# Two layers of a hybrid backbone on one core: where chunks, weight blocks and late queries stand in the order of the program

## The chip, the cores and the metric

The program runs on one core of one Trainium2 chip. The metric is the time of one execution on the device, in microseconds; the medians below are of three timed runs. One further execution was taken with the hardware profiler, and all rows below come from it.

## The reference

It computes two layers on 1024 latent tokens and 128 context tokens of width 1024, 1152 in all. Each layer normalizes its input, scales and shifts it by values from a conditioning vector, runs a mixer, and adds the gated, normalized result to the input. Cut to the names that matter:

```python
def even_mixer(h, w_in, ...):            # layer 0
    p = h @ w_in
    qa, ka, va, oa, gates, qb, kb, vb, z = split(p)
    ha = rmsnorm(mlstm(qa, ka, va, gates, forward) + mlstm(..., backward)) * sigmoid(oa)   # 4 heads of 128
    hb = block_attend(rope(rmsnorm(qb)), [rope(rmsnorm(kb)), ctx_k], [vb, ctx_v])          # 8 query heads of 64 over 2 key heads
    return (concat(ha, hb) * silu(z)) @ w_out

def odd_mixer(h, w_in, rpb, w_out, ...): # layer 1
    q, k, v, z = split(h @ w_in)         # 16 heads of 64
    o = na_attend(q, k, v, ctx_k, ctx_v, rpb)   # 8 x 16 window of the grid and all context keys, one softmax
    return (o * silu(z)) @ w_out

for layer in range(2):
    h = rmsnorm(x) * (1 + scale) + shift
    x = x + gate * rmsnorm(mixer(h))
```

The outputs are both token groups after the two layers, the mLSTM states, and the keys and values of the context.

## The kernel before

**Tiling.** The 1152 tokens are three chunks of 384 columns (`CW`), the width of 1024 eight blocks of 128 (`KB`). Each operand of the projections is split into a high and a low part (`hh`, `hl` for activations, `whi`, `wlo` for weights), and a product is three matmuls per k: high by high, high weights by low activations, low weights by high activations. `feat_part` (L362 to L369) issues these for one chunk; a block of 128 output columns for one chunk is a group of 24 matmuls of 384 columns in one PSUM bank, then evicted by one of the functions `evs` (q, k, v, o, z). The 16 gates of the mLSTM have their own group of 16 matmuls (`gates_proj`, L395 to L417).

**Buffers.** SBUF tiles of one tag rotate. Almost everything large has the tag "u", a pool of 35 slots: activations, weight halves, queries, bias tables, softmax rows. Raw weights land in two "raw" buffers, are cast by ScalarE (ACT) to `whi`, and GpSimd (POOL) or VectorE (DVE) subtracts to get `wlo` (`weights`, L121; `split`, L110). The PSUM banks are: pj two, s three, and tr, ptr and o one each.

**Order.** A planner orders the instructions of each engine by a simulated time, with the order of tracing as priority; the grouped-query attention alone has TensorE's order written out by hand. Slots of a tag are given out in the order of tracing, so what is traced earlier has its slots earlier. DMAs wait in SP's queue, or in that of another engine, in order.

**Phases.** *front*: for k = 0 to 7 the modulation of block k (`mod_first`), the normalization of chunk 0's block k (`norm_cols`) and then, for chunk 0, the gates and four weight blocks of head 0 (q, k, v, o), each in an own bank (`acc`: o, three of s, tr). The column statistics (`rms_cols`, L286 to L312) of chunk 1 are computed at k = 5, those of chunk 2 after the loop. `later(c, bs)` then computes blocks bs of chunk c in the pj banks, block 0 being the gates. *a*: the gate chain (`gates`, L419 and after: transposes, cumulative sums and maxima of the gates over all tokens, a pass through DRAM, exponentials into `e`), the rest of head 0, its z block and head 1's first blocks. *mlstm*: four heads. *g*: queries, keys and values of the grouped-query attention, `gqa_q` (L851). *gqa*: units of two query tiles, ten turns of transposes each (`gqa_turn`), apply, gate; `w_out(0, k)` is loaded between. *out0*: output projection of layer 0 and the normalization for layer 1; it loads y back from DRAM through the raw buffers (`load_y`). *na*: eight pairs of heads, `na_proj(p)` (projections) and `na_pair(p)` (attention, nine units); blocks in `late` are projections of the same pair that are put between its units. Pairs 1, 3 and 5 compute the values of two pairs at once from `w_v`. The last part of the output projection runs beside pair 7.

**Names of the change.** `turned` (L871) transposes the queries of one tile and casts them; for the second group g = 1 the calls of tiles 7 and 8 are put off into `self.turned` and popped in the first unit of `gqa`. `w_out(l, j)` (L1075) loads a block of the output weights; its second argument to `weights` says which engine subtracts ("lo" is DVE, "" is POOL). `W(b)` in `na_proj` (L1114) loads block b of pair p (0 q, 1 k, 2 v, 3 z).

## Time and profile before

| | us |
|---|---|
| median of three timed runs (lowest and highest 1527.02 and 1527.52) | 1527.03 |
| the profiled execution | 1527.66 |
| its span, first to last instruction | 1525.9 |
| PE busy in the span | 1489.1 |
| PE weight loads busy | 1370.8 |
| DVE busy | 828.0 |
| ACT busy | 711.9 |
| POOL busy | 449.3 |

The span is the profiler's time from the first to the last instruction; 1.76 us of that execution lie outside. Busy times are sums of durations of each engine; weight loads run beside matmuls. A matmul's end is modelled, so that durations of matmuls that follow each other overlap. In a timeline row the bracket gives the idle time of the engine before the instruction and the instruction or DMA that ended it.

### The profile page before, as it was taken

To read this page: it belongs to the slowest core of one execution; us is meant where nothing else is said; L and a number is where in the kernel's file an instruction comes from. 1 tells how busy PE (TensorE), PEld (TensorE's weight loads), DVE (VectorE), ACT (ScalarE), POOL (GpSimd) and SP (SyncE) were. 2 spreads that over 40 slices of the span, in tenths; PEclk is the share of its full clock that TensorE was granted. 3 is DMA by queue.
4 is the path that set the end of the run, shared out by engine and by line. 5 is a ranking of instruction groups with operands and counts; after the bars stand their busy time and mean duration, and the time that the engine had idled before them with its cause. 6 is when DMAs were issued, how large, how long until landed. Compare 5 with 4: busy or idle time off the path is not lost.

```text
span 1525.9 us, 27070 instructions
## 1 busy us (share of the span) xinstructions
PE 1489.1 (98%) x10139; PEld 1370.8 (90%) x10139; DVE 828.0 (54%) x2387; ACT 711.9 (47%) x1767; POOL 449.3 (29%) x644
## 2 busy tenths in 40 slices
PE   7899999999999999999999999999999999999998
PEld 5799999999999888887888989999999999988786
DVE  5833887963457766665565352535344434445532
ACT  4533535263445777786454352534344344345411
POOL 0001202011135655675224141323132222233200
PEclk9999999999999999999999999999999999999999
DMA  9203546332311000122423222131213121125342
GB/s 378 79 15 130 190 147 239 137 122 75 111 48 44 1 32 24 44 67 70 151 98 137 74 62 80 42 98 31 85 38 104 33 82 69 54 90 167 106 131 83
DMA packets 73284, 143.80 MB, mean 94 GB/s; under 512 B 15737, under 2 KB 44609, under 8 KB 73153
## 3 DMA queue, kind: packets, MB, share of 16 engines
q1 hardware_dynamic: 68566, 126.91, 25.0%
q10 hardware_dynamic: 4586, 15.16, 2.7%
q8 instruction: 80, 1.31, 0.3%
q14 instruction: 52, 0.42, 0.1%
HBM read 115.47 MB, written 21.86 MB: 90 GB/s over the span
## 4 chain that ended last, share of the span: by engine, by line
PE 49%; DMA 1%; DVE 1%; ACT 1%; POOL 1%; issue 0%; DVEq 0%; POOLq 0%; ACTq 0%
PE pj L367 7%; PE pj L368 7%; PE pj L369 7%; PE pj L383 6%; PE pj L382 6%; PE pj L384 6%; PE o L1290 4%; PE s L1267 3%; PE ptr L107 2%; PE tr L107 2%; DMA y<-yd 1%; POOL wlo L116 1%; DMA raw<-in_w_out_dram 0%; DVE sb L1273 0%; POOL pr L925 0%
## 5 line engine op out<-in xcount | busy, mean ns | idle before, releaser
L367 PE MATMUL pj<-hh,whi 128*128 128x384 f32 x1168 | 400.2, 343 | 1.8 <-ACT qT L102 1.2
L368 PE MATMUL pj<-hl,whi 128*128 128x384 f32 x1168 | 397.0, 340 | 0.0
L369 PE MATMUL pj<-hh,wlo 128*128 128x384 f32 x1168 | 395.8, 339 | 0.5 <-DVE wlo L116 0.4
L367 PEld LDWEIGHTS pj<-hh,whi 128*128 128x128 f32 x1168 | 219.6, 188 | 5.5 <-ACT qT L102 1.8
L369 PEld LDWEIGHTS pj<-hh,wlo 128*128 128x128 f32 x1168 | 219.4, 188 | 1.9 <-DVE wlo L116 0.9
L368 PEld LDWEIGHTS pj<-hl,whi 128*128 128x128 f32 x1168 | 219.6, 188 | 1.2
L1277 POOL TENSOR_SCALAR sb<-sb,sm 128x512 f32<-128x512 f32 (+1 forms) x128 | 85.1, 671 | 247.7 <-DVE sm L1276 238.7
L116 POOL TENSOR_TENSOR wlo<-raw,whi 128x1024 fp32r<-128x1024 f32 x43 | 103.0, 2400 | 132.8 <-ACT whi L115 113.7
L925 POOL TENSOR_SCALAR pr<-pr,smg 128x384 f32<-128x384 f32 x192 | 110.0, 591 | 73.9 <-PE pj L107 41.0
L382 PE MATMUL pj<-whi,hh 128*128 128x256 f32 x432 | 122.5, 284 | 0.3 <-DVE nr L783 0.3
L383 PE MATMUL pj<-wlo,hh 128*128 128x256 f32 x432 | 122.5, 284 | 0.0
L384 PE MATMUL pj<-whi,hl 128*128 128x256 f32 x432 | 122.2, 283 | 0.0
L382 PE MATMUL pj<-whi,yh 128*128 128x512 f32 x288 | 114.3, 397 | 2.9 <-DVE o L1085 1.5
L916 DVE CUSTOM_DVE_ANT_0 pr<-s,zero 128x384 f32<-128x384 f32 x192 | 103.8, 553 | 24.3 <-PE s L915 20.9
L383 PE MATMUL pj<-wlo,yh 128*128 128x512 f32 x288 | 113.9, 395 | 0.0
L1275 ACT ACTIVATE sb<-sb,sm 128x512 f32<-128x512 f32 (+1 forms) x128 | 88.9, 695 | 52.9 <-DVE sm L1273 49.3
L384 PE MATMUL pj<-whi,yl 128*128 128x512 f32 x288 | 113.3, 394 | 0.0
L915 PE MATMUL s<-Kst,Q 128*128 128x384 f32 x384 | 107.8, 372 | 1.1 <-ACT pt L1035 1.1
L254 DVE CUSTOM_DVE_ANT_0 mj<-wm,cb 128x512 f32<-128x512 f32 x128 | 89.5, 699 | 5.2 <-DMA wm<-in_w_modT_dram 3.0
L115 ACT CAST whi<-raw 128x1024 fp32r<-128x1024 f32 x77 | 79.7, 1046 | 19.5 <-DMA raw<-in_w_v_dram 6.6
L1273 DVE CUSTOM_DVE_ANT_1 sb<-s,bias 128x512 f32<-128x512 f32 (+1 forms) x112 | 72.9, 664 | 24.9 <-PE ptr L107 12.1
L382 PEld LDWEIGHTS pj<-whi,hh 128*128 128x128 f32 x432 | 81.3, 188 | 1.4 <-issue 0.5
(350 smaller groups left out, 2901.3 us busy)
## 6 DMA issues: line engine op xcount, KB each, us to landing
wm<-in_w_modT_dram SPq DMA_DIRECT2D x32, 512.0 KB, 5.2
raw<-in_w_c_dram SPq DMA_DIRECT2D x25, 512.0 KB, 3.5
raw<-in_w_ab_dram SPq DMA_DIRECT2D x20, 512.0 KB, 3.5
e<-rbd ACTq DMA_DIRECT2D x12, 768.0 KB, 7.7
bias<-in_na_bias_dram SPq DMA_DIRECT2D x16, 576.0 KB, 4.1
wm<-in_w_mod_dram SPq DMA_DIRECT2D x16, 512.0 KB, 9.8
raw<-in_w_out_dram SPq DMA_DIRECT2D x16, 512.0 KB, 3.6
y<-yd SPq DMA_DIRECT2D x18, 448.0 KB, 3.4
```

The lines of the kernel that those rows point to most:

```text
L116: (eng_lo or nc.gpsimd).tensor_tensor(lo, src, hi.bitcast(F32), ALU.subtract)
L254: nc.vector.tensor_tensor_reduce(junk, w[:, b, :], cb[:, r, :], 1.0, 0.0, ALU.mult, ALU.add, mp[:, hf, q // 4, 2 * (q % 4) + b, r : r + 1])
L367: nc.tensor.matmul(ps[:, :CW], a, hh, start=k == 0, stop=False)
L368: nc.tensor.matmul(ps[:, :CW], a, hl, start=False, stop=False)
L369: nc.tensor.matmul(ps[:, :CW], b, hh, start=False, stop=k == KB - 1)
L382: nc.tensor.matmul(ps[:, :width], hh, a, start=k == 0, stop=False)
L383: nc.tensor.matmul(ps[:, :width], hh, b, start=False, stop=False)
L384: nc.tensor.matmul(ps[:, :width], hl, a, start=False, stop=k == KB - 1)
L915: nc.tensor.matmul(s[:, :CW], x, y, start=part == 0, stop=part == 1)
L916: nc.vector.tensor_tensor_reduce(pr[:, c, :], s[:, :CW], zero, -1.0, -NEG, ALU.add, ALU.min, m3[:, c : c + 1])
L925: nc.gpsimd.tensor_scalar(pr[:, c, :], pr[:, c, :], r, 0.5, ALU.mult, ALU.mult)
L1275: nc.scalar.activation(x, x, AF.Exp, bias=nm, scale=-1.0, accum_out=r)
```

## The change

It has five parts.

1. *Front.* In the per-k loop chunk 0 has three weight blocks instead of four. After the loop chunk 1's gates and q block are computed in two passes, k = 0 to 3 for both, then k = 4 to 7 for both, each in a pj bank. Then chunk 0's fourth block (o) is computed in its bank, then k, v and o of chunk 1, then the gates of chunk 2; in phase a q and k of chunk 2, then v and o. Before, the order was gates, q, k of chunk 1, gates of chunk 2, in phase a q and k of chunk 2, v of both chunks, o of both. `rms_cols` of chunk 2 is traced after the rest of `norm_cols` of chunk 1 instead of ahead of it.
2. *Late queries.* `turned` of tiles 7 and 8 of the second group takes a bank of tag s instead of ptr or tr, and the two calls are popped at turns 7 and 9 of the first unit instead of 5 and 7.
3. *Output weights of layer 0.* For j = 6 and 7 DVE subtracts instead of POOL.
4. *Values of pair 1.* The two weight blocks of `w_v` are loaded and split at the end of `na_proj(0)`, ahead of `na_pair(0)`, instead of in `na_proj(1)`.
5. *Pair 7.* Blocks v, q and z of pair 7 are loaded and split at the end of `na_proj(6)`, ahead of `na_pair(6)`, instead of in `na_proj(7)`.

```diff
--- before.py
+++ after.py
@@ -869,7 +869,7 @@
                 Q.append(self.u([P, 2, 4, P], F32R, n="Q"))
 
             def turned(i=i, q=q, Qt=Q[-1]):
-                pt = self.ps(("tr", "ptr")[i % 2])[:, :256]
+                pt = self.ps("s" if g and i in (7, 8) else ("tr", "ptr")[i % 2])[:, :256]
                 for j in range(2):
                     self.flipped(pt[:, j * P : (j + 1) * P], q[:, 2 * j : 2 * j + 2].rearrange("p a b -> p (a b)"))
                 for hh in range(2):
@@ -994,7 +994,7 @@
                 next(steps, None)
                 next(steps, None)
                 for n, _ in enumerate(turns):
-                    if (j, i, n) in ((0, 0, 5), (0, 0, 7)):
+                    if (j, i, n) in ((0, 0, 7), (0, 0, 9)):
                         self.turned.pop(0)()
                     if i == 4 and n == 7 or i == 6 and n == 5:
                         next(ctx)
@@ -1074,7 +1074,7 @@
 
     def w_out(self, l, j):
 
-        return self.weights(self.a["w_out"][l, j], ("", "lo")[j % 2] if l else "")
+        return self.weights(self.a["w_out"][l, j], "lo" if (j % 2 if l else j >= 6) else "")
 
     def out_half(self, y, w, n, o, ss, gg):
         nc = self.nc
@@ -1109,9 +1109,12 @@
             self.nc.sync.dma_start(raw, self.a["w_c"][4 * p + b])
         return self.weights(self.a["w_c"][4 * p + b], raw=raw)
 
+    def v_weights(self, p):
+        return [self.weights(self.a["w_v"][p // 2, :, q * D : (q + 1) * D]) for q in range(2)]
+
     def na_proj(self, h, p, w):
         nc, a = self.nc, self.a
-        W = lambda b: self.na_weights(p, b)
+        W = lambda b: self.w7[b] if p == 7 and b in self.w7 else self.na_weights(p, b)
         two = lambda t: t[2 * p : 2 * p + 2].rearrange("h t d -> t h d")
         v2 = lambda t: t.rearrange("p (h d) -> p h d", d=DHB)
 
@@ -1181,7 +1184,7 @@
             self.feat(h, W(2), vev)
         elif p % 2:
 
-            w = [self.weights(a["w_v"][p // 2, :, q * D : (q + 1) * D]) for q in range(2)]
+            w = self.wv if p == 1 else self.v_weights(p)
             for i in range(NT):
                 ps = self.tok(h, i, lambda k: tuple(x[:, (k % 4) * 256 : (k % 4 + 1) * 256] for x in w[k // 4]), 256)
                 nc.scalar.copy(v[:, i, :], ps[:, :P])
@@ -1211,6 +1214,11 @@
             self.feat(h, w, kev)
 
             late = [lambda w=w, e=e, c=c: self.feat(h, w, e, [c]) for w, e, c in [(wq, qev, 2), (wz, zev, 2)]]
+
+        if p == 0:
+            self.wv = self.v_weights(1)
+        if p == 6:
+            self.w7 = {b: self.na_weights(7, b) for b in (2, 0, 3)}
 
         def terms(hh, j, k0, n):
 
@@ -1357,7 +1365,7 @@
                 if k + 1 < KB:
                     self.mod_first(k + 1, wm[k + 1])
                 self.norm_cols(h, 0, xt[0], rms[0], [k])
-                for b in range(NB + 1):
+                for b in range(3 + 1):
                     part[b](acc[b], 0, [k])
 
                 if k == 5:
@@ -1365,10 +1373,10 @@
                 if k > 5:
                     self.norm_cols(h, 1, xt[1], rms[1], range(3 * k - 18, 3 * k - 15))
             ends = [gend, *evs[:NB]]
-            for b in range(NB + 1):
+            for b in range(3 + 1):
                 ends[b](0, acc[b][:, :CW])
+            self.norm_cols(h, 1, xt[1], rms[1], range(6, KB))
             rms.append(self.rms_cols(xt[2]))
-            self.norm_cols(h, 1, xt[1], rms[1], range(6, KB))
             self.norm_cols(h, 2, xt[2], rms[2], range(KB))
 
             def later(c, bs):
@@ -1377,16 +1385,23 @@
                     part[b](ps, c, range(KB))
                     ends[b](c, ps[:, :CW])
 
-            later(1, (0, 1, 2))
+            ps = [self.ps("pj") for _ in range(2)]
+            for ks in (range(KB // 2), range(KB // 2, KB)):
+                for b in range(2):
+                    part[b](ps[b], 1, ks)
+            for b in range(2):
+                ends[b](1, ps[b][:, :CW])
+            for b in range(3 + 1, NB + 1):
+                part[b](acc[b], 0, range(KB))
+                ends[b](0, acc[b][:, :CW])
+            later(1, (2, 3, 4))
             later(2, (0,))
         with self.phase("a"):
             self.gates(gT)
             self.c0 = [self.load_c0(hd) for hd in range(2)]
             self.nall = self.const([P, 8], "nall")
             later(2, (1, 2))
-            for b in range(3, NB + 1):
-                for c in (1, 2):
-                    later(c, (b,))
+            later(2, (3, 4))
             blocks(0, evs, (4,), lambda n: self.t(n, 1, [P, D], F32R))
             nxt, evs = self.mlstm_proj(1)
             blocks(1, evs, (0, 1))
```

## Rows read from the trace of the kernel before

**Rows 1.** The page, busy time of each engine over the span: us, share, instructions.

```profile
PE 1489.1 (98%) x10139; PEld 1370.8 (90%) x10139; DVE 828.0 (54%) x2387; ACT 711.9 (47%) x1767; POOL 449.3 (29%) x644
```

**Rows 2.** The table of stretches: window, its length in us, then the busy us of PE, PEld, DVE, ACT and POOL with their instructions, the granted clock of PE, the share of the DMA engines and GB/s. The first is the later half of the front, the second the start of grouped-query attention.

```profile
61.00:75.00 14.00, 12.38 (x69) 10.87 (x69) 12.98 (x40) 8.24 (x21) 0.00 (x0) 1.00 0.05 10
...
514.00:524.00 10.00, 6.52 (x48) 5.05 (x48) 6.71 (x26) 9.58 (x21) 7.83 (x14) 1.00 0.00 0
```

**Rows 3.** The timeline of PE in the front, 49 to 75 us: start, duration, engine, line, operation, out<-in, form and count, and in brackets the idle time before it and what ended it.

```profile
49.62 0.33 PE L368 MATMUL pj<-hl,whi 128*128 128x384 f32 x1
...
49.80 0.34 PE L369 MATMUL pj<-hh,wlo 128*128 128x384 f32 x1
...
51.67 0.39 PE L408 MATMUL o<-hh,wg 128*64 128x384 f32 x1 [1.54 <-ACT hh L325]
...
53.61 0.39 PE L409 MATMUL o<-hl,wg 128*64 128x384 f32 x1 [0.50 <-DVE hl L326]
...
60.77 0.45 PE L367 MATMUL pj<-hh,whi 128*128 128x384 f32 x1 [0.39 <-ACT qT L102]
...
69.84 0.39 PE L409 MATMUL pj<-hl,wg 128*64 128x384 f32 x1 [0.80 <-DVE hl L326]
...
74.02 0.45 PE L367 MATMUL pj<-hh,whi 128*128 128x384 f32 x1 [0.81 <-ACT qT L102]
```

**Rows 4.** The timeline of DVE in the front, 47 to 76 us, columns as in rows 3: a step of the column statistics (L299), the second half of the gates' eviction (L415), and a run of the normalization of chunk 2 (L326).

```profile
48.03 1.35 DVE L299 TENSOR_TENSOR s<-s,s 128x1152 f32<-128x1152 f32 x1
...
60.25 0.55 DVE L415 TENSOR_TENSOR gT<-pj,cross 16x384 f32<-16x384 f32 x1 [1.53 <-ACT cross L413]
...
69.05 2.72 DVE L326 SCALAR_TENSOR_TENSOR hl<-full,mod,hh 128x256 fp32r<-128x256 f32 x8
```

**Rows 5.** The gate chain in the timelines of PE, ACT and DVE: its first step on PE, the last of its exponentials on ACT, and the first use of e on DVE.

```profile
74.92 0.66 PE L432 MATMUL tr<-cc,gT 16*128 16x16 f32 x8
...
129.91 1.87 ACT L650 ACTIVATE e<-e,nat 128x128 f32<-128x128 f32 x6 [1.01 <-DMA e<-rbd]
...
139.67 0.95 DVE L704 TENSOR_TENSOR e<-e,s 128x768 f32<-128x768 f32 x1 [3.41 <-PE s L703]
```

**Rows 6.** The timelines of PE and ACT at the start of grouped-query attention, 514 to 524 us: the two late query transposes, and one eviction of pt.

```profile
519.71 0.41 PE L107 MATMUL ptr<-cc,nr 128*128 128x128 f32 x2 [0.95 <-ACT pt L946]
...
522.44 0.41 PE L107 MATMUL tr<-cc,nr 128*128 128x128 f32 x2 [1.45 <-ACT pt L946]
...
521.22 0.59 ACT L946 COPY pt<-pj 128x512 f32<-128x512 f32 x1
```

**Rows 7.** One subtraction of wlo on DVE in phase a (118.74), and then the last w_out block and the load of y in the timelines of ACT, POOL, SP (DMA issues) and PE, 703 to 718 us.

```profile
118.74 1.23 DVE L116 TENSOR_TENSOR wlo<-raw,whi 128x1024 fp32r<-128x1024 f32 x1 [2.35 <-ACT whi L115]
...
705.37 1.06 ACT L115 CAST whi<-raw 128x1024 fp32r<-128x1024 f32 x1
...
709.45 2.37 POOL L116 TENSOR_TENSOR wlo<-raw,whi 128x1024 fp32r<-128x1024 f32 x1
...
711.85 11.51 SPq L1064 DMA_DIRECT2D y<-yd  x3
...
715.31 0.94 ACT L115 CAST yh<-y 128x896 fp32r<-128x896 f32 x1 [4.08 <-DMA y<-yd]
...
716.30 0.50 PE L382 MATMUL pj<-whi,yh 128*128 128x512 f32 x1 [1.33 <-ACT yh L115]
```

**Rows 8.** Pair 0 in the timelines of PE, SP, DVE and ACT, 840 to 912 us: three stalls of PE, the load and the cast of the weights of V for pair 1, the write of a pt slot ahead of the cast, and two matmuls of that V projection which follow each other.

```profile
880.36 0.47 PE L1267 MATMUL s<-k,q 128*128 128x512 f32 x1 [0.99 <-DVE sm L1276]
...
881.95 0.47 PE L1267 MATMUL s<-k,q 128*128 128x512 f32 x1 [0.49 <-DVE sm L1276]
...
887.98 0.48 PE L1267 MATMUL s<-k,q 128*128 128x512 f32 x1 [0.97 <-issue]
...
844.99 0.34 SPq L126 DMA_DIRECT2D raw<-in_w_v_dram  x1
...
883.74 0.69 DVE L104 COPY pt<-tr 128x512 f32<-128x512 f32 x1
...
884.18 1.05 ACT L115 CAST whi<-raw 128x1024 fp32r<-128x1024 f32 x1
...
911.57 0.28 PE L382 MATMUL pj<-whi,hh 128*128 128x256 f32 x1
...
911.69 0.28 PE L383 MATMUL pj<-wlo,hh 128*128 128x256 f32 x1
```

**Rows 9.** Pair 6 in the timelines of PE and ACT, 1318 to 1355 us: its first scores, four stalls of PE, and the cast of the next weights of pair 7.

```profile
1318.09 0.34 PE L1267 MATMUL s<-k,q 128*128 128x384 f32 x1
...
1345.57 0.33 PE L1031 MATMUL s<-k,q 128*128 128x128 f32 x1 [0.63 <-DVE sm L1273]
...
1347.65 0.44 PE L1290 MATMUL o<-pt,v 128*64 128x128 f32 x4 [0.28 <-ACT pt L102]
...
1351.84 0.52 PE L107 MATMUL ptr<-cc,sb 128*128 128x128 f32 x3 [0.44 <-ACT pt L102]
...
1352.93 0.55 PE L107 MATMUL ptr<-cc,vT 128*128 128x128 f32 x3 [0.35 <-ACT pt L102]
...
1352.77 1.99 ACT L115 CAST whi<-raw 128x1024 fp32r<-128x1024 f32 x2
```

**Rows 10.** The page's table of DMA issues, the bias tables of the neighbourhood attention: count, KB each, median us from issue to landing.

```profile
bias<-in_na_bias_dram SPq DMA_DIRECT2D x16, 576.0 KB, 4.1
```

## The prediction

> **What bounds the kernel now.** The page's table of busy time comes first: TensorE (PE) is busy for 98% of the span, VectorE (DVE) for 54% and ScalarE (ACT) for 47% [rows 1]. So the question for every edit is whether PE stands still at that place, and for how long. A matmul's duration doesn't say that, since its end is modelled: two matmuls of 384 columns that follow each other start 0.18 us apart (49.62 and 49.80), though each shows 0.33 or 0.34 us [rows 3]. Where PE stalls, the idle column leaves out the part that the modelled end covers: from 49.80 to the next start at 51.67 are 1.87 us, less 0.18 a stall of 1.69, where the column has 1.54 [rows 3]. I add 0.15 to each idle figure for this reason.
>
> So I read PE's timeline, not the shares, and looked for gaps in the stretches that the diff touches. The rows show them: five in the front, two at the start of grouped-query attention, one at the first output projection, several in the pairs 0 and 6 of the neighbourhood attention [rows 3, 6 to 9]. Together the idle columns of the 15 gaps in those rows make 11.9 us; with 0.15 for each, 14.2. No edit removes PE work: that sum is nearly all that there is to gain.
>
> **Front (chunk order).** Nothing is removed; 24 matmuls per group only change places. The idle columns are 1.54, 0.50, 0.39, 0.80 and 0.81, sum 4.04, with 5 x 0.15 it is 4.8 [rows 3]. The first two wait for hh and hl of chunk 0's last k: PE has run dry. Taking the fourth block out of the per-k loop takes work from PE there, so that it runs dry earlier at each k, and what is put off doesn't help before the loop's end in trace order. Unless the planner fills in with it, the two stay, and the work moved behind them only gives back what it took; I credit 0.4 of their 2.3. The next three wait for qT's eviction or for hl of chunk 2. Then DVE is busy 12.98 of 14 us [rows 2], with 2.72 us of hl in one run [rows 4], and both pj banks are held by groups of chunk 2 that need it. The change puts 48 matmuls of chunk 1 (v and o, 48 x 0.18 = 8.6 us) in that place, all of whose inputs are there. Those three (2.00 + 0.45 = 2.45) I take as nearly gone: 2.1. Front: 2.5, bounds 0 and 4.8. That rms_cols of chunk 2 goes behind norm_cols of chunk 1 lets the latter have DVE first; PE has the put-off o block (4.3 us) as cover. Without it the statistics' 1.35 us step on DVE [rows 4] would come late to chunk 2's gates, which the gate chain pays (below).
>
> The two-pass groups hold both pj banks till their ends. The 60.77 gap shows what this costs: PE waits for qT, whose eviction stands behind that of the gates, of which gT on DVE took 0.55 [rows 3, 4]. The Trainium skill ("Perfetto Trace Analysis", Matmuls) wants independent groups to rotate through PSUM banks so that the evacuation of one overlaps the next group. By that rule the two-pass form keeps an eviction of some 0.55 in the open and the front gives 2.0, the total 0.5 less. I don't follow it here, since the o block that is next has a bank of its own; no row of the kernel before shows the new order.
>
> **Late queries in s banks.** The two turned() calls wait for an eviction of pt on ACT: idle 0.95 and 1.45, with 2 x 0.15 it is 2.7 [rows 6]. With a bank of tag s they need none of the banks of gqa_turn. But ACT is busy 9.58 of 10 us there [rows 2], each eviction takes 0.59 [rows 6], and every pt still has to leave before the apply. Popped two turns later, the four Q casts also come later, and whoever uses query tiles 7 and 8 waits longer; that use is several units on. PE work comes forward, ACT's doesn't. I take 2.0; bounds 0.5 (only one of the gaps shrinks) and 2.7.
>
> **wlo on DVE.** POOL's subtraction for the last w_out block runs 709.45 to 711.82 and holds the raw buffer; at 711.85 SP issues the load of y, ACT casts yh at 715.31, and PE starts at 716.30 after 1.33 idle [rows 7]. The cast that it needs was done at 705.37 + 1.06 = 706.43, and on DVE the same form took 1.23 [rows 7]: the buffer is free at some 708 to 709, about 3 us sooner. Behind the two subtractions on DVE stand evictions of pt that PE's apply waits for; 1.23 each is the price if they are caught in a row, and PE's score and transpose work of that stretch is the cover. The gap with its 0.15 is 1.5, less than the 3 us; what is late next is the last key block of y, which comes from the apply itself. I take 1.4; bounds 0 (the evictions come late by as much) and 1.5.
>
> **Weights of V for pair 1.** In pair 0 PE waits 0.99, 0.49 and 0.97 [rows 8], mostly for DVE's softmax sums: nothing else is ready. With 3 x 0.15 that is 2.9. V's raw weights were issued at 844.99 but cast at 884.18, right after a write to a pt slot at 883.74 [rows 8]: slots are given out in trace order. Traced ahead of na_pair(0), weights and their 9 x 24 matmuls (0.12 apart [rows 8], 26 us) are filler for the whole pair. What is next: two pj banks, whose evictions write v and v2, slots traced later, so that the filler may stop after two groups (48 x 0.12 = 5.8 us). This still covers three gaps. I take 2.5; bounds 0.5 (one small gap) and 2.9, in which the third is the least sure, since it has "issue" as its releaser.
>
> **Weights of pair 7.** In pair 6 the gaps are 0.63, 0.28, 0.44 and 0.35, with 4 x 0.15 it is 2.3 [rows 9]. They stand where the late blocks are used up, and pair 7's weights are cast only at 1352.77 [rows 9]. Traced ahead, V's 24-matmul groups of pair 7 are at hand, again two banks of them (8.6 us). Against it: six more slots of the 35 are taken before pair 6's bias tables; by my count one of the tables must then wait till pair 6's key weights are done, at 1318.09 [rows 9], and takes 4.1 us to land [rows 10]. First scores of head two would be 4 us late with the filler of V7 as cover; without this cover it costs up to 1 us of PE beyond what is won. I take 1.8; bounds -1 and 2.3.
>
> **Sum.** 2.5 + 2.0 + 1.4 + 2.5 + 1.8 = 10.2 us. The profiled execution took 1527.66 us, of which 1525.9 are the span and 1.76 lie around it; 1527.66 - 10.2 = 1517.5. The median of the timed runs, 1527.03, is 0.63 below the profiled one: 1516.8 on that scale. By the idle column alone the ceiling would be 11.9, by starts 14.2. The Trainium skill ("Perfetto Trace Analysis", Identifying the Most-Contended Engine) says that TensorE's busy share is no good measure since its instructions are pipelined; rows 3 agree with it (0.34 shown, 0.18 apart), which is why I count by starts.
>
> **Rivals.** (1) *The stalls move instead of going.* DVE and ACT set the supply in the front, in the turns and in the pairs; 12.98 of 14 and 9.58 of 10 us speak for it [rows 2], the whole span's 54% and 47% against it [rows 1]. Then the front keeps 0.8, the queries 1.0, wlo 1.4, V 1.2 and pair 7 0.5, in all 4.9: 1527.03 - 4.9 = 1522.1. (2) *The weights ahead find no slot.* The change doesn't do what it says if the pool of 35 is full at both new places; for it speaks that slots go out in trace order and that the cast stood behind a pt slot [rows 8]; against, that one write alone stood between: the cast followed it at once. Then 2.5 + 2.0 + 1.4 = 5.9: 1521.1. (3) *The gate chain comes late: slower.* Chunk 2's gates are now traced behind v and o of chunk 1, where before they had only chunk 2's q beside them: 24 matmuls more, 4.3 us, less the 2.5 of the front, so that the chain that starts at 74.92 [rows 5] comes 1.8 later. It has some eight steps on PE, and each can find itself behind a group of 24 (4.3 us). Its end is e, exponentiated until 129.91 + 1.87 = 131.78 and used at 139.67 [rows 5], a slack of 7.9; less 1.8, and less 2.5 since mLSTM now comes sooner, 3.6. If four steps slip by a group, 17.2 - 3.6 = 13.6 are lost against the 10.2 won: 3.4 slower, 1530.4. It decides from a slip of 13.8, more than three groups. Against it: the planner puts the chain first where it can, and DVE's wait of 3.41 before that use is for PE's scores, not for e [rows 5].
>
> **How the numbers follow.** Forecast 0.62; rival 1 0.18; rival 2 0.09; rival 3 0.07; the rest, 0.04, for gains near the ceiling of 14.2 (1512.8) or beyond, since the planner reorders more than the diff says. The terms' low bounds, 0 + 0.5 + 0 + 0.5 - 1 = 0, are not all reached at once; their high ones make that ceiling. The range 1511 to 1523.5 holds forecast, rivals 1 and 2 and the ceiling; it leaves out rival 3 and the tails. 0.2% (3.05 us) is about what a measurement can tell from no change: faster is below 1523.98. Faster 0.84 (the forecast, most of rivals 1 and 2), same 0.09, slower 0.07.
>
> **What would show it.** Right: no gap over 0.3 between 60 and 76 and none on a pt eviction at 518 to 524; SP issues the last y load before PE ends its apply; V's first cast for pair 1 stands before 870 and pair 7's before 1330. Wrong: PE waits for o's or q's eviction after the two passes; the same DVE waits in pairs 0 and 6 with casts ahead (rival 1); casts where they were (rival 2); a PE gap at 135 to 146 whose releaser is e (rival 3). A shorter kernel whose named gaps all stay would refute the whole working.

## The result and the profile after

The changed kernel takes 1516.96 us (median of six runs, 1515.95 to 1518.21); the kernel before, on the same chips, 1527.16 (six runs, 1526.24 to 1529.14). The ratio is 0.9932, with a 95% interval of 0.9919 to 0.9945: faster by some 10 us, against the 1516.8 us of the prediction. Two executions of all that were timed took 3793 and 5216 us, far from the others of the same kernels; they are left out of every figure below. The profiled execution of the changed kernel took 1517.28 us, with a span of 1515.6.

The page of the changed kernel, span and busy times, beside [rows 1]:

```profile
span 1515.6 us, 27083 instructions
PE 1487.5 (98%) x10139; PEld 1373.2 (91%) x10139; DVE 827.2 (55%) x2389; ACT 711.9 (47%) x1767; POOL 445.8 (29%) x642
```

PE has the same number of matmuls in a span that is 10.3 us shorter, and its busy share still reads 98%: the share doesn't show the gain, the gaps do. Since the order of work within a stretch differs, I compare stretches between the same matmuls of each trace, in us: from the first gates matmul of chunk 0 (L408 into o), by the first scores (L915) and the first apply (L955) of the grouped-query attention, the last yh product of layer 0's output projection (L382) and the first scores of pair 1 (L1267, after the change L1275), to the last matmul.

| stretch | before | after | front undone | queries undone | wlo undone | V undone | pair 7 undone |
|---|---|---|---|---|---|---|---|
| first gates to first scores | 439.62 | 437.30 | **439.77** | 437.41 | 437.38 | 437.33 | 437.38 |
| to first apply | 61.10 | 58.34 | 58.37 | **61.12** | 58.36 | 58.39 | 58.35 |
| to end of output projection | 297.73 | 297.40 | 297.49 | 297.27 | **297.81** | 296.87 | 297.16 |
| to pair 1 | 128.34 | 124.69 | 124.66 | 124.71 | 124.66 | **128.50** | 124.68 |
| to last matmul | 569.62 | 567.79 | 567.51 | 567.76 | 567.97 | 568.22 | **569.74** |

(The right five are the runs of the next section.) The five stretches of the changed kernel are 2.32, 2.76, 0.33, 3.65 and 1.83 shorter, 10.89 in all; its first gates matmul came 0.55 later (23.39 after 22.84), which isn't the change's, as this start lies between 22.06 and 23.46 in the traces of all versions that have the same instructions ahead of it. That leaves the 10.3 us. Each stretch comes from one execution. The cells that an edit doesn't touch show how far to trust them: the right five agree within 0.1 in the first, second and fourth row, and within 0.6 and 0.7 in the third and the last.

**Front.** The timeline of PE in the changed kernel, 48 to 82 us: the same two gaps near 50 us and the one at 60 as in [rows 3], the last matmul of chunk 0's o block (into tr, at 55.62), the two gaps near 70 and 74 gone, and the first step of the gate chain:

```profile
52.22 0.39 PE L408 MATMUL o<-hh,wg 128*64 128x384 f32 x1 [1.54 <-ACT hh L325]
54.16 0.39 PE L409 MATMUL o<-hl,wg 128*64 128x384 f32 x1 [0.50 <-DVE hl L326]
55.62 0.33 PE L369 MATMUL tr<-hh,wlo 128*128 128x384 f32 x1
61.33 0.44 PE L367 MATMUL pj<-hh,whi 128*128 128x384 f32 x1 [0.44 <-ACT qT L102]
81.07 0.72 PE L432 MATMUL tr<-cc,gT 16*128 16x16 f32 x9
```

The o block is not late on the chip: the planner put its 24 matmuls back into the loop, where they start between 24.15 and 55.62, as they did between 23.61 and 55.08 in the kernel before. The gate chain starts 6.2 us later than in [rows 5] (81.07 after 74.92). Its end, in the timelines of ACT, POOL, DVE and PE of the changed kernel, 130 to 140 us:

```profile
134.56 1.87 ACT L650 ACTIVATE e<-e,nat 128x128 f32<-128x128 f32 x6 [1.52 <-DMA e<-rbd]
136.50 0.52 POOL L651 TENSOR_SCALAR_AFFINE_SELECT e<-e 128x384 f32<-128x384 f32 x1 [0.35 <-ACT e L650]
137.82 0.95 DVE L704 TENSOR_TENSOR e<-e,s 128x768 f32<-128x768 f32 x1
138.82 0.71 PE L710 MATMUL s<-v,e 128*128 128x129 f32 x4 [0.79 <-DVE e L704]
```

e is exponentiated 4.65 us later than before and used 1.85 us sooner. POOL's mask (L651), which the prediction had left out of the chain, ends at 136.50 + 0.52 = 137.02; DVE uses e at 137.82. In the kernel before the same mask ended at 132.37, so that of the 7.9 us that looked like slack 7.3 were there; 0.8 are left.

**Late queries.** PE of the changed kernel, up to the first apply. Both transposes of nr stand in a row of work without a gap, where [rows 6] had 0.95 and 1.45:

```profile
517.85 0.38 PE L107 MATMUL s<-cc,nr 128*128 128x128 f32 x2
518.06 0.60 PE L107 MATMUL pj<-cc,pr 128*128 128x128 f32 x4
...
518.72 0.38 PE L107 MATMUL s<-cc,nr 128*128 128x128 f32 x2
```

**Output projection.** PE of the changed kernel, 706 to 712 us: no gap before the first product, beside [rows 7]; but two products now stand inside the last apply, and the context's apply (L1050) is cut in two:

```profile
706.02 3.24 PE L955 MATMUL o<-pt,V 128*64 128x256 f32 x26
709.19 0.50 PE L382 MATMUL pj<-whi,yh 128*128 128x512 f32 x1
709.53 0.40 PE L383 MATMUL pj<-wlo,yh 128*128 128x512 f32 x1
709.85 1.29 PE L955 MATMUL o<-pt,V 128*64 128x256 f32 x9
710.77 0.38 PE L1050 MATMUL s<-pt,VP 128*64 128x128 f32 x2
...
711.20 0.38 PE L1050 MATMUL s<-pt,VP 128*64 128x128 f32 x2
711.51 0.50 PE L384 MATMUL pj<-whi,yl 128*128 128x512 f32 x1
```

**Pairs 0 and 6.** ACT of the changed kernel casts the first of V's weights for pair 1 as the second of two casts from 852.48 on (with V undone there is one, from 851.00) and the other at 859.59, both over 24 us ahead of the cast in [rows 8]; pair 7's q and z are cast at 1295 and 1297 instead of 1352.77 [rows 9]:

```profile
852.48 2.00 ACT L115 CAST whi<-raw 128x1024 fp32r<-128x1024 f32 x2
859.59 1.05 ACT L115 CAST whi<-raw 128x1024 fp32r<-128x1024 f32 x1 [2.09 <-DMA raw<-in_w_v_dram]
...
1294.95 1.05 ACT L115 CAST whi<-raw 128x1024 fp32r<-128x1024 f32 x1 [2.73 <-DMA raw<-in_w_c_dram]
1297.37 1.05 ACT L115 CAST whi<-raw 128x1024 fp32r<-128x1024 f32 x1 [1.36 <-DMA raw<-in_w_c_dram]
```

PE of the changed kernel has no gap left in pair 0 at the place of [rows 8]. Of the four of [rows 9] in pair 6, two are gone and two stay:

```profile
1350.52 0.52 PE L107 MATMUL ptr<-cc,sb 128*128 128x128 f32 x3 [0.44 <-ACT pt L102]
1351.61 0.55 PE L107 MATMUL ptr<-cc,vT 128*128 128x128 f32 x3 [0.35 <-ACT pt L102]
```

### The profile page after: what moved, and what is told of

It reads as the page before. It is cut to its first block, busy times and chain, and to the rows that moved or that the text cites. A ratio compares the mean times of both kernels' runs of the same rounds, so it can differ in the third digit from the quotient of the medians.

```text
span 1515.6 us, 27083 instructions
## 1 busy us (share of the span) xinstructions
PE 1487.5 (98%) x10139; PEld 1373.2 (91%) x10139; DVE 827.2 (55%) x2389; ACT 711.9 (47%) x1767; POOL 445.8 (29%) x642
## 4 chain that ended last, share of the span: by engine, by line
PE 50%; DMA 1%; ACT 1%; DVE 1%; issue 0%; DVEq 0%; POOLq 0%; POOL 0%; ACTq 0%
PE pj L367 7%; PE pj L368 7%; PE pj L369 7%; PE pj L382 6%; PE pj L383 6%; PE pj L384 6%; PE s L1275 4%; PE o L1298 4%; PE ptr L107 2%; PE tr L107 2%; DMA y<-yd 1%; ACT yh L115 0%; DVE yl L116 0%; DVE wlo L116 0%; PE o L1050 0%
## 5 line engine op out<-in xcount | busy, mean ns | idle before, releaser
L116 POOL TENSOR_TENSOR wlo<-raw,whi 128x1024 fp32r<-128x1024 f32 x41 | 98.3, 2402 | 127.8 <-ACT whi L115 108.3
L382 PE MATMUL pj<-whi,hh 128*128 128x256 f32 x432 | 123.0, 285 | 0.3 <-DVE nr L783 0.3
L382 PE MATMUL pj<-whi,yh 128*128 128x512 f32 x288 | 114.5, 398 | 1.8 <-DVE o L1085 1.5
L915 PE MATMUL s<-Kst,Q 128*128 128x384 f32 x384 | 107.9, 372 | 1.1 <-ACT pt L1035 1.1
L382 PEld LDWEIGHTS pj<-whi,hh 128*128 128x128 f32 x432 | 81.4, 188 | 1.5 <-issue 0.6
## 6 DMA issues: line engine op xcount, KB each, us to landing
wm<-in_w_mod_dram SPq DMA_DIRECT2D x16, 512.0 KB, 10.1
```

The lines of the kernel that those rows point to most:

```text
L116: (eng_lo or nc.gpsimd).tensor_tensor(lo, src, hi.bitcast(F32), ALU.subtract)
L382: nc.tensor.matmul(ps[:, :width], hh, a, start=k == 0, stop=False)
L915: nc.tensor.matmul(s[:, :CW], x, y, start=part == 0, stop=part == 1)
```

## The experiments

Each kernel is the changed one with the edit shown. A profile goes with each; the median is of four runs (six for the late gates, three for `w7_v`), beside medians of the kernel before of 1527.30, 1527.76 and 1527.01 in the three sets. Single runs of one kernel lie up to 5 us apart (7 with the late gates), so that the stretches between the same matmuls decide where an edit of under 1 us went, and the medians only confirm.

### The five parts, each undone

`u_front`: the per-k loop with four blocks, no two passes, statistics first, and the block order as before.

```diff
-                for b in range(3 + 1):
+                for b in range(NB + 1):
                     part[b](acc[b], 0, [k])
...
-            later(1, (2, 3, 4))
+            later(1, (0, 1, 2))
             later(2, (0,))
...
             later(2, (1, 2))
-            later(2, (3, 4))
+            for b in range(3, NB + 1):
+                for c in (1, 2):
+                    later(c, (b,))
```

> The changed kernel with part 1 (the front) undone, parts 2 to 5 kept. Theory of the places (each part is worth the gaps of TensorE at its own place, nothing else moves): by the two traces the second mLSTM chunk comes 1.8 us earlier in the changed kernel, so this one should take 1517.0 + 1.8 = 1518.8, with the gaps of 0.80 and 0.81 near 70 and 74 us back. The prediction's term says 2.5, so 1519.5. Rival, the gate chain eats the front's gain (the chain starts 6.2 us later in the changed kernel): undoing the front costs under 0.5, so about 1517.

Measured: 1518.85 us (1518.31 to 1519.73). PE's timeline of this kernel has the gaps near 70 and 74 us back, and one more in the mLSTM:

```profile
71.15 0.39 PE L409 MATMUL pj<-hl,wg 128*64 128x384 f32 x1 [0.80 <-DVE hl L326]
75.32 0.44 PE L367 MATMUL pj<-hh,whi 128*128 128x384 f32 x1 [0.81 <-ACT qT L102]
...
166.40 0.44 PE L369 MATMUL pj<-hh,wlo 128*128 128x384 f32 x1 [0.42 <-DVE wlo L116]
```

By the stretch the front is worth 439.77 - 437.30 = 2.47. The gaps of 0.80 and 0.81 with 0.15 each are 1.91 of it. The gap of 0.42 at 166.40, a wait for wlo that the kernel before has too (0.42 at 165.11) and the changed kernel lacks, makes 0.57 with its 0.15: 2.48 together. The rival, a chain that eats the gain, is out.

The granted clock could blur this comparison, since each of the two executions has one fall in this stretch: to 0.50 from 54 to 57 us here, to 0.51 from 144 to 147 in the changed kernel (last section). Up to the same scores of the mLSTM (at 197.34 in the changed kernel) the two need 176.41 and 173.95 us from the first gates matmul. The kernel before and `t_split`, which has the changed front, show no fall there and need 174.84 and 172.44. The front is worth 2.4 to 2.5 either way.

`u_turned`: the banks ptr and tr again, pops at turns 5 and 7.

```diff
-                pt = self.ps("s" if g and i in (7, 8) else ("tr", "ptr")[i % 2])[:, :256]
+                pt = self.ps(("tr", "ptr")[i % 2])[:, :256]
...
-                    if (j, i, n) in ((0, 0, 7), (0, 0, 9)):
+                    if (j, i, n) in ((0, 0, 5), (0, 0, 7)):
```

> The changed kernel with part 2 (late queries) undone. Theory of the places: 2.75 us later from the first apply on, 1519.7, with both gaps on a pt eviction (0.95 and 1.45) back. The prediction's term: 2.0, so 1519.0. Rival, ScalarE's supply binds anyway: 1.0 or less, 1518.0.

Measured: 1518.94 us (1518.30 to 1520.53); the stretch to the first apply is 61.12 again, 2.78 longer, and both gaps are back:

```profile
517.00 0.41 PE L107 MATMUL ptr<-cc,nr 128*128 128x128 f32 x2 [0.99 <-POOL pr L925]
519.73 0.41 PE L107 MATMUL tr<-cc,nr 128*128 128x128 f32 x2 [1.45 <-ACT pt L946]
```

The part is worth the whole of its two gaps.

`u_wout`: POOL subtracts for all blocks of layer 0.

```diff
-        return self.weights(self.a["w_out"][l, j], "lo" if (j % 2 if l else j >= 6) else "")
+        return self.weights(self.a["w_out"][l, j], ("", "lo")[j % 2] if l else "")
```

> The changed kernel with part 3 (wlo of the last two output blocks on DVE) undone. The prediction's term: 1.4, so 1518.4. Theory of the broken pairs: the planner put two matmuls of the output projection into the last apply, whose matmuls otherwise run in pairs on the two column halves; that gives back 0.9 of the 1.6 us gap, and a new gap of 0.40 at 722 us more, so undoing the part costs only 0.4: 1517.4.

Measured: 1517.94 us (1517.37 to 1520.39). PE's timeline, 705 to 712 us:

```profile
705.65 4.11 PE L955 MATMUL o<-pt,V 128*64 128x256 f32 x36
...
711.29 0.50 PE L382 MATMUL pj<-whi,yh 128*128 128x512 f32 x1 [1.32 <-ACT yh L115]
```

The gap of 1.32 is back and the 36 matmuls of the apply stand together again. The stretch is 0.41 longer than in the changed kernel. The other versions with part 3, `c_manual` aside, lie between 296.87 (V undone) and 297.49 (front undone). A short gap before 722.68 in the changed kernel (0.40 by starts) doesn't account for that spread: `t_split` lacks it and has the same 297.40. So the part is worth 0.3 to 0.9, not the gap's 1.5.

`u_v1`: V's weights of pair 1 again in `na_proj(1)`.

```diff
-            w = self.wv if p == 1 else self.v_weights(p)
+            w = self.v_weights(p)
...
-        if p == 0:
-            self.wv = self.v_weights(1)
```

> The changed kernel with part 4 (weights of V for pair 1 ahead) undone. Theory of the places: between the end of the output projection and pair 1's first scores the changed kernel wins 3.65 us, so 1520.6, with the gaps of 0.99, 0.49 and 0.97 back. The prediction's term: 2.5, so 1519.5. Rival, DVE's softmax sums bind: 1.2 or less, 1518.2.

Measured: 1519.96 us (1517.03 to 1520.32). The table of stretches of this kernel and of the changed one, the same 19 us of each (columns as in [rows 2]):

```profile
866.00:885.00 19.00, 16.37 (x97) 13.63 (x95) 11.44 (x37) 11.65 (x27) 9.51 (x10) 1.00 0.21 57
```

```profile
866.00:885.00 19.00, 19.00 (x127) 17.74 (x126) 10.12 (x34) 9.35 (x23) 4.34 (x7) 1.00 0.18 46
```

With V ahead PE is busy for all of the 19 us, without it for 16.37, and starts 97 matmuls in place of 127. The stretch to pair 1 is 3.81 longer. The three gaps of [rows 8] are back (0.99, 0.49 and 0.97), with two short ones of 0.08 and 0.10 among them: 3.4 with 0.15 for each. The last 0.4 isn't traced. DVE, the engine that PE waited for, has 11.4 and 10.1 of 19 us of work: it set when each score unit went on, not how much PE could do in between.

`u_w7`: q, z and v of pair 7 again in `na_proj(7)`.

```diff
-        W = lambda b: self.w7[b] if p == 7 and b in self.w7 else self.na_weights(p, b)
+        W = lambda b: self.na_weights(p, b)
...
-        if p == 6:
-            self.w7 = {b: self.na_weights(7, b) for b in (2, 0, 3)}
```

> The changed kernel with part 5 (weights of pair 7 ahead) undone. Theory of the places: 2.3 us later from pair 7's last scores on, 1519.2, with the gaps of 0.63 and 0.28 in pair 6 back. The prediction's term: 1.8, so 1518.8. Rival, a late bias table costs what the filler wins: 1517.

Measured: 1518.77 us (1516.55 to 1520.85); the last stretch is 1.95 longer. In pair 6 the gaps of 0.63 and 0.28 are back, and in pair 7 one that the prediction didn't name:

```profile
1402.44 0.63 PE L107 MATMUL tr<-cc,sb 128*128 128x128 f32 x4 [0.61 <-DVE pt L104]
```

The kernel before has it too (0.44 at 1411.14), the changed one doesn't. The three make 1.97 with 0.15 for each; why the third goes isn't shown. The rival's bias table does come late in the changed kernel. SP's queue there:

```profile
1298.93 0.38 SPq L1238 DMA_DIRECT2D bias<-in_na_bias_dram  x1
1309.61 0.33 SPq L1238 DMA_DIRECT2D bias<-in_na_bias_dram  x1
```

The second table is issued just as pair 6's first scores start (1309.60), as the prediction counted, but the filler covers it. (The row of 1318.09 in [rows 9] is the second head's; the first scores of pair 6 in the kernel before are at 1313.52.)

### What in the front, and in pair 6, did it

`f_oloop`: chunk 0's o block back in the per-k loop; `f_order`: the whole front as before, with only the order of blocks changed.

```diff
-                for b in range(3 + 1):
+                for b in range(NB + 1):
                     part[b](acc[b], 0, [k])
...
-            for b in range(3 + 1, NB + 1):
-                part[b](acc[b], 0, range(KB))
-                ends[b](0, acc[b][:, :CW])
```

> The changed kernel, but chunk 0's o block goes back into the per-k loop; the two passes and the new block order stay. The prediction took the late o block to be worth 0.4 at the two gaps near 50 us, which the changed kernel still has (1.55 and 0.51): then 1517.4, and the gaps of 70 and 74 us stay closed since the order of the blocks closes them. Rival, the late o block is what fills the place around 60 us: then a gap of over 1 us opens between 60 and 75 and the time is 1518.5 or more.

Measured: 1516.45 us (1515.92 to 1517.94), first stretch 437.25 against 437.30, and the gaps at 70 and 74 us stay closed. This says nothing of a late o block, since neither kernel has one: o's 24 matmuls start between 23.83 and 55.29 here, between 24.15 and 55.62 in the changed kernel.

```diff
...
-            self.norm_cols(h, 1, xt[1], rms[1], range(6, KB))
             rms.append(self.rms_cols(xt[2]))
+            self.norm_cols(h, 1, xt[1], rms[1], range(6, KB))
...
-            ps = [self.ps("pj") for _ in range(2)]
-            for ks in (range(KB // 2), range(KB // 2, KB)):
...
-            later(1, (2, 3, 4))
+            later(1, (0, 1, 2, 3, 4))
             later(2, (0,))
```

> The changed kernel with the front as before (four blocks in the per-k loop, no two passes, the statistics of chunk 2 first) except for the order of the blocks: gates, q, k, v and o of chunk 1, then the gates of chunk 2, then q, k, v, o of chunk 2. Theory of the order: the ready v and o blocks of chunk 1 alone close the gaps near 70 and 74 us, so 1516.5 to 1517. Rival, the two passes or the place of the statistics are needed: one of the two gaps (0.96 or 0.98 by starts) stays or the 60 us gap grows, 1518 or more.

Measured: 1517.51 us (1515.99 to 1518.37), first stretch 437.60. PE's timeline, 49 to 78 us, has these gaps and no other:

```profile
51.88 0.39 PE L408 MATMUL o<-hh,wg 128*64 128x384 f32 x1 [1.54 <-ACT hh L325]
53.82 0.39 PE L409 MATMUL o<-hl,wg 128*64 128x384 f32 x1 [0.50 <-DVE hl L326]
60.97 0.45 PE L367 MATMUL pj<-hh,whi 128*128 128x384 f32 x1 [0.39 <-ACT qT L102]
```

By the stretch the order of the blocks brings 439.77 - 437.60 = 2.2 of the front's 2.47; the rest is within what this stretch varies (436.66 in `c_manual` and 437.58 in `t_split`, whose front is the same program). Up to the mLSTM's scores it is 172.29 us against the 172.44 of `t_split`, with no fall of the clock in either: the order is all of it. The other three edits hardly reach the engines. The planner fits the gates and q of chunk 1 together as their inputs arrive, with and without the two passes, and DVE's steps of statistics and normalization follow each other alike up to 61 us.

`f_gates_late`: gates of chunk 2 and the chain behind q and k of chunk 2.

```diff
-            later(2, (0,))
         with self.phase("a"):
+            later(2, (1, 2))
+            later(2, (0,))
             self.gates(gT)
...
-            later(2, (1, 2))
             later(2, (3, 4))
```

> The changed kernel, but the gates of chunk 2 and the gate chain are traced behind the q and k blocks of chunk 2 (48 matmuls, 8.6 us later). Theory of the used-up slack: in the changed kernel the first e is ready 0.8 us before its use, so nearly all of the delay beyond that shows as TensorE gaps before the first mLSTM products, 5 us or more lost, 1522 or later, if no other projection is at hand. Rival, the slack of 7.9 us that the prediction read from the kernel before is still there: 1 us or less lost, 1518.

Measured: 1522.79 us (six runs, 1522.14 to 1529.17), 5.8 above the changed kernel; the first stretch is 443.62, 6.3 longer. The chain's first step is at 90.14, and PE's timeline, 134 to 146 us, has gaps of 1.43, 0.57, 0.57 and 1.32:

```profile
139.01 0.55 PE L107 MATMUL ptr<-cc,kT 128*128 128x128 f32 x3 [1.43 <-ACT kT L585]
140.13 0.55 PE L107 MATMUL ptr<-cc,kT 128*128 128x128 f32 x3 [0.57 <-ACT k L102]
142.60 0.69 PE L107 MATMUL ptr<-cc,c 128*128 128x128 f32 x2 [0.57 <-ACT k L102]
144.62 1.23 PE L666 MATMUL o<-v,kw 128*128 128x129 f32 x4 [1.32 <-DVE cs L673]
```

The four make 3.89, where the changed kernel has 0.79, 0.79, 0.57 and 0.39 (2.54) in the same place. And the granted clock falls behind them. The table of stretches of this kernel, and then of the changed one (columns as in [rows 2]):

```profile
141.00:144.00 3.00, 1.61 (x7) 0.62 (x6) 1.60 (x5) 2.74 (x9) 0.26 (x1) 0.60 0.99 336
144.00:147.00 3.00, 2.38 (x9) 2.20 (x9) 2.66 (x6) 3.00 (x9) 1.30 (x3) 0.50 0.66 274
```

```profile
141.00:144.00 3.00, 1.72 (x8) 1.08 (x9) 1.35 (x5) 2.05 (x5) 0.99 (x3) 0.92 0.00 0
144.00:147.00 3.00, 3.00 (x14) 3.00 (x15) 1.81 (x5) 0.22 (x1) 0.00 (x0) 0.51 0.23 27
```

The chain's slack is used up, as the 0.8 us in the changed kernel say. More and wider gaps and a longer time at the low clock (0.50, the level of 1.2 GHz) are what the delay turned into; how the 6.3 us divide between them isn't shown. (This execution's clock is low in the front too, 0.63 from 54 to 57 us, ahead of the edit. The executions of `u_wout` and `w7_v` also have such a fall, and their first stretches are 437.38 and 437.36.) The third rival's mechanism is real; to outweigh the 10.9 us of the five stretches it would have taken nearly twice this loss.

`f_gates_early`: the same gates ahead of chunk 1's o block.

```diff
-            later(1, (2, 3, 4))
+            later(1, (2, 3))
             later(2, (0,))
+            later(1, (4,))
```

> The changed kernel with the gates of chunk 2 ahead of chunk 1's o block instead of behind it, so that the gate chain starts up to 4.2 us sooner. If the used-up slack of the chain costs the changed kernel anything (first products of the mLSTM wait 0.98 for e, 0.5 more than before), the gain is 0.5 and no gap opens near 70 us: 1516.5. Rival, the gates of chunk 2 come before DVE has their inputs: the 0.96 gap near 70 us is back and the time is 1517.5.

Measured: 1516.41 us (1515.91 to 1517.73), but not for the reason expected: the chain's first step is at 81.50, no sooner than 81.07, e makes PE wait as long as before, and the first stretch is 437.97, with a gap of 0.40 at 77.27 for an eviction and the wait of 0.42 for wlo back (165.39). The gates were traced earlier but the chain didn't start earlier, so the run tells nothing of the slack.

`t_split`: the s banks, but the pops at turns 5 and 7.

```diff
-                    if (j, i, n) in ((0, 0, 7), (0, 0, 9)):
+                    if (j, i, n) in ((0, 0, 5), (0, 0, 7)):
```

> The changed kernel with the two late queries in s banks but popped at turns 5 and 7 as before. Theory of the bank: the wait was for the bank that a pt eviction held, so the bank alone gives all of the 2.8 us: 1517.0. Rival, the turn: ScalarE's evictions and casts still stand in the way two turns earlier, half or more of the 2.8 comes back, 1518.4 to 1519.

Measured: 1516.76 us (1516.44 to 1517.35), stretch to the first apply 58.16 against 58.34. The bank is all of it, the turn nothing.

`w7_v`: only v of pair 7 ahead.

```diff
-            self.w7 = {b: self.na_weights(7, b) for b in (2, 0, 3)}
+            self.w7 = {b: self.na_weights(7, b) for b in (2,)}
```

> The changed kernel with only block v of pair 7 traced ahead (q and z as before), so four slots fewer are held in pair 6. Theory of the filler: V7's matmuls alone cover the gaps of 0.80 and 0.48 (by starts) in pair 6, and both bias tables of pair 6 are issued together again: 1517.0. Rival, q's and z's matmuls do part of the covering: 0.5 to 2 later, 1517.5 to 1519.

Measured: 1518.05 us (1516.62 to 1518.09); the last stretch is 570.26, as long as with the part undone. ACT and PE of this kernel:

```profile
1342.86 2.00 ACT L115 CAST whi<-raw 128x1024 fp32r<-128x1024 f32 x2
```

```profile
1335.66 0.33 PE L1031 MATMUL s<-k,q 128*128 128x128 f32 x1 [0.64 <-DVE sm L1281]
1337.74 0.44 PE L1298 MATMUL o<-pt,v 128*64 128x128 f32 x4 [0.28 <-ACT pt L102]
1341.93 0.52 PE L107 MATMUL ptr<-cc,sb 128*128 128x128 f32 x3 [0.44 <-ACT pt L102]
1343.02 0.55 PE L107 MATMUL ptr<-cc,vT 128*128 128x128 f32 x3 [0.35 <-ACT pt L102]
```

All four gaps of [rows 9] are there, and so is the one in pair 7 (0.65 at 1401.57). V7's 72 matmuls stood beside pair 6 already in the kernel before (between 1319.6 and 1337.1 us); what the changed kernel adds are two groups, 48 matmuls, that wait for the q and z weights. Counting the projection matmuls of pair 7 beside pair 6 gives 120 in the changed kernel and 72 in this one.

### The apply and its strangers

`c_manual`: the hand-written order of PE goes on over the first half row of the output projection.

```diff
-            with self.tc.manual_schedule(engines={mybir.EngineType.PE}):
-                last = self.gqa(Q, gz, early, ahead)
+            by_hand = self.tc.manual_schedule(engines={mybir.EngineType.PE})
+            by_hand.__enter__()
+            last = self.gqa(Q, gz, early, ahead)
...
                         self.out_half(ys[i], w, n, o, ss, gg[i // 8])
+                        if i == 0 and n == 0:
+                            by_hand.__exit__(None, None, None)
```

> The changed kernel, but the hand-written order of TensorE goes on over the first half row of the output projection, so that none of its matmuls stands inside the last apply. Theory of the broken pairs: the apply's last 36 matmuls take 3.9 us again instead of 5.0 with the two strangers among them, and the first output matmul still starts without a gap: 0.7 us less, 1516.3. Rival, the extra time is a wait for yl and not the pairs: no gain, and a gap of that size before the first group, 1517.

Measured: 1516.17 us (1514.62 to 1516.55). PE's timeline, 705 to 711 us:

```profile
705.46 4.28 PE L955 MATMUL o<-pt,V 128*64 128x256 f32 x36
709.40 0.56 PE L1050 MATMUL s<-pt,VP 128*64 128x128 f32 x4
709.89 0.50 PE L382 MATMUL pj<-whi,yh 128*128 128x512 f32 x1
```

From the start of the apply to the first product are 4.43 us. In the changed kernel 706.02 to 711.51 are 5.49 with two strangers in it, which here take 0.57 (709.89 to 710.46): 0.5 us for the broken pairs and the changes between apply and projection. The stretch to the end of the output projection is 0.93 shorter than in the changed kernel and 0.4 shorter than in any other version. The interval of the ratio to the kernel before, 0.9907 to 0.9939, overlaps with that of the changed kernel, so the runs don't tell the two apart as whole kernels. It has the lowest median of all that ran.

## Why the prediction was right

The time, 1516.8 against 1516.96, is closer than its terms were: errors of both signs cancelled, and that is luck: three of the five terms were off by 0.5 to 1.3.

- **Front, 2.5: measured 2.3 to 2.5.** The size was right, its parts not. I credited 0.4 at the two gaps near 50 us and part of 60; all three stay. The gaps near 70 and 74 us went entirely, by the order of the blocks alone, and 0.57 came from a wait for wlo at 165 us that I hadn't listed. The Trainium skill ("Perfetto Trace Analysis", Matmuls) wants independent groups to rotate through PSUM banks, so that the evacuation of one overlaps the next. By that rule the two passes leave an eviction open (0.55 by [rows 4]). My reason against it failed: the o block that was to stand next had already run, and PE waits 0.44 for q's eviction. But it waited 0.39 before, and 0.38 with the two passes in `f_oloop`; since the two groups run in nearly the same order with and without the passes, no run here tests the rule.
- **Late queries, 2.0: measured 2.8,** just over the upper bound of 2.7. The reduction for ScalarE's supply was wrong. ACT was busy for 9.58 of 10 us, but what PE waited for was the bank (`t_split`), and the evictions that remain are in time.
- **wlo, 1.4: measured 0.3 to 0.9.** The gap went, as worked out. What took its place wasn't the next wait that I named, but PE's own order: products that were ready early were put between the two halves of an apply.
- **V, 2.5: measured 3.7 to 3.8,** well over the upper bound of 2.9. The three gaps that I counted make 2.9; the table of stretches shows PE without any idle time in their place, and two shorter gaps that I hadn't listed went too. Some 0.4 stays open.
- **Pair 7, 1.8: measured 1.8 to 1.9.** Right in size by luck, wrong in its source. I named V's groups as the filler; they had been there before, and q's and z's two groups fill two of the four gaps, 1.2 with 0.15 for each. The other two (0.44 and 0.35) are after these groups and stay. The rest is the gap in pair 7 that I hadn't named.
- **Rivals.** The first (stalls move) shows in wlo alone. The second is out: the casts moved forward at both places. The third was nearer than its price said: the chain came 6.2 us later, not 1.8. From the first gates matmul to its start are 216 matmuls of weight blocks after 172, so 44 more where I had counted 24, and POOL's mask, which I had overlooked, is part of it. It was covered with 0.8 us to spare; 9.1 us more of delay cost 5.8.
- **Signs.** One of the signs of being right failed: the gap of 0.44 at 61.33 is over 0.3, and it is the wait for q's eviction that I had named as a sign of being wrong. The others held: no wait for pt at the late queries, y's load issued at 703.24, before the apply ends, casts ahead at both places. The third rival's sign, a gap that e ends, stands in the trace (0.79 at 138.82 and at 141.32), but the kernel before has it too (0.32 at 140.68 and 0.79 at 143.18), so it tells little.

## What to carry to other kernels

Where one engine is busy nearly all the time, list its gaps, find for each what ready work the program already holds, and ask only whether that work's inputs and banks can be there: five such lists gave 10 us of 1527 here. A group that is ready beats a group whose turn it is: the order of two blocks brought all that the front gained. Where a planner stands between the program and the engines, look in the trace whether an edit arrived: the late block and the two passes never did. And test each part by undoing it, since a total that fits doesn't mean that its terms do.

## What the hardware showed that was not expected

Two apply matmuls on the two column halves (L955, 64 output rows each, tile positions 0 and 64) run side by side: in the order by hand the two of most pairs start 0.01 us apart and the next pair 0.21 later, and 36 of them take 3.94 us from the first start (705.46) to that of L1050 (709.40), 0.22 for two. A half without its partner takes as long: in the changed kernel two stand alone ahead of the strangers (708.66 and 708.88), 0.22 apart. The stretch with two strangers took 5.49 us, against 4.43 and 0.57 for the same work in order.

TensorE's granted clock goes down behind the gaps at 138 to 144 us, to 0.51 between 144 and 147 in the changed kernel (about the level of 1.2 GHz), after PE was busy for 1.72 of the 3 us before. It needn't: in the profiled execution with the pops at turns 5 and 7, whose front is the same program, this row reads

```profile
144.00:147.00 3.00, 3.00 (x23) 3.00 (x22) 1.87 (x4) 0.69 (x2) 0.00 (x0) 1.00 0.21 29
```

with 23 instructions of PE in place of 14. Up to 140 us the same matmuls start within 0.2 us of each other in both; the mLSTM's scores at 197.34 in the changed kernel start at 195.66 in that execution, 1.7 ahead; at the first scores of the grouped-query attention it is 0.1 behind (460.79 against 460.69). So the fall cost some 1.5 us at its place and nothing at the end of the phase. The lead goes between 259 and 280 us, through a load: DVE of that execution idles 3.30 us until e has landed (257.06; the last load of e before it was issued at 249.15), and PE waits 0.85 for hs at 266.96. In the changed kernel that load was issued at 250.86, DVE went on at 256.32 after 0.85, and PE has no gap there. Why the one load took longer isn't shown.

In the executions of `u_front`, `u_wout`, `w7_v` and `f_gates_late` the clock falls in the front, behind the gaps of 1.54 and 0.50 near 50 us: to 0.50, 0.50, 0.57 and 0.63 from 54 to 57 us, where PE starts 11 to 13 matmuls; the changed kernel and the kernel before, with the same gaps, stay at 1.00 there, with 16 and 20.

The first gates matmul starts at 22.06 us in one trace and at 23.46 in another, with the same program up to there, and this stays: with the queries undone it came 1.05 sooner than in the changed kernel, and the first scores of the grouped-query attention still 0.95 sooner (459.74 against 460.69).
